# Later transposes of the routing's results, and one-hot operands made one token group ahead, in an expert layer on one core

## The chip, the core and the metric

The kernel runs on 1 core of one Trainium2 chip. The metric is the device time of one execution in microseconds (us), median of several runs. Engines are named as in the profile: PE is TensorE's matmuls and PEld its weight loads, DVE is VectorE, ACT is ScalarE, POOL is GpSimd, SP is SyncE, which issues the weight transfers here.

## The reference

Two transformer layers on one sequence of 256 tokens with 1,024 features. What matters here is the last part, an expert layer with 16,384 experts, of which each token uses 16 for each of 8 heads:

```
q = (h @ w_query).reshape(B, S, 8, 2, 128)
s1, s2 = q[..., 0, :] @ sub_keys1.T, q[..., 1, :] @ sub_keys2.T
v1, i1 = top_k(s1, 16);  v2, i2 = top_k(s2, 16)
cand = v1[..., :, None] + v2[..., None, :]       # 256 candidates
top_v, pos = top_k(cand, 16)
expert_idx = (i1 * 128 + i2) at pos              # routing's places
gates = softmax(top_v)
act = gelu(h . expert_down[expert_idx])
out = sum(gates * act * expert_up[expert_idx])
```

## The kernel before

The kernel computes the expert layer densely: every expert for every token, with a gate that is zero for experts a token did not choose. `peer` runs two stages. The stage of `down` has 64 pairs `jj` of expert tiles; a pair is 2 tiles of 128 experts, each contracted over 8 blocks of features. `mm3` writes three matmuls for each block (L96, L97, L98: high part by high, by low, and low by high), so a pair has 48 matmuls named `dn`. The stage of `up` follows, 128 tiles into four accumulators (`upp`).

Weights are streamed. SP loads a tile (`eraw`, 512 KB), ACT casts it to the high half (`whi`, L69), DVE subtracts to get the low half (`wlo`, L71), four times for a pair. The pool of `whi` and `wlo` has 4 buffers each, which is one pair. `g.mark` is the last of the first 12 `dn` matmuls of the newest pair.

Between the pairs two other things are issued by the Python loop at the end of `peer`. While `routing` lasts, each pair is followed by three steps of that generator. For each of the 8 heads it makes scores (`sps`), the two top-16 lists and the 256 candidates' top 16 on DVE (L1156 to L1204), and puts the two halves of the places into `gts[tt]` (`rk`, L1204), where `tt` is one of the two halves of the tokens. After the last head, for each `tt`, it makes the softmax (L1210 to L1215), and then, once a further pair has been issued, three transposes on PE (`slp`, L1223). ACT and DVE copy them into `slots` as 16-bit numbers (L1225 to L1227): places i1 and i2, and the gate in a high and a low part.

When `routing` has ended, each pair is followed by one or two calls of `gates()`. A call treats a group of NG = 8 tokens, 32 groups in all. It makes `eq` (two instructions, L1301: is this slot's place equal to j) and `gt` (two, L1303: the second of them times the gate) on DVE, 128x1024 each and 16 bits wide, from pools with 2 buffers. It then multiplies them on PE (`gps`, L1309, 16 matmuls into two PSUM tiles of 4 tokens), which gives the gates of all experts for those tokens. For expert tiles that `down` has already done, DVE multiplies the gates into `act` (L1314). For the others, ACT copies them there (L1316), and a later `down` multiplies (L1283, L1284).

`dn`, `gps`, `slp` and `sps` share the PSUM pool `aux` with 5 buffers. A planner fixes each engine's order of instructions when the program is built (`schedule_with_timeline_sim=True`): it follows its own estimate of when each instruction becomes ready, and `after(...)` only gives it an order to keep.

The pairs at which things are issued follow from the code. A head takes 12 steps, that is 4 pairs, so the heads' steps end after pair 30. The softmax of `tt` = 0 is issued after pair 31, its transposes after pair 32; the softmax of `tt` = 1 after pair 32, its transposes after pair 33. Gates start after pair 34: two calls after each of the pairs 34, 35 and 36, one after each of the pairs 37 to 62.

Of the kernel before, what the change touches and what calls it, by code (L numbers as in the profile page):

```python
# [20 lines left out]
T = 256  # L21
# [118 lines left out]
def after(g, ins, first):  # L140

    g.tc.add_manual_dep(ins, first.name, mybir.DependencyInfo(mybir.DependencyClass.NoSync, mybir.DependencyReason.DATA),
                        reason="table order")
# [10 lines left out]
def load(g, dst, src):  # L154

    after(g, g.nc.sync.dma_start(dst, src).ins, g.pm)
# [932 lines left out]
def advance(gen, n):  # L1089

    return sum(next(gen, g) is not g for g in [gen] * n) > 0
# [49 lines left out]
def routing(g, a, q_banks, rp, cp, slots):  # L1141

    nc = g.nc

    rk = rp.tile([P, 1296], F32, tag="rk", name="rk")
    keys = rk[:, 0:256].rearrange("p (a b) -> p a b", a=2)
    io16 = rk[:, 256:272]
    val = [rk[:, 272 + t * 128:400 + t * 128].rearrange("p (a b) -> p a b", a=8) for t in range(2)]  # L1150
    gts = [rk[:, 528 + t * 384:912 + t * 384].rearrange("p (a b) -> p a b", a=3) for t in range(2)]
    load(g, keys, a["keys"])
    load(g, io16, a["c_io16"])

    def top16(src, n, v, i):
        nc.vector.max(v[:, 0:8], src)  # L1156
        nc.vector.max_index(i[:, 0:8], v[:, 0:8], src)
        r = rp.tile([P, 256], F32, tag="rep", bufs=2, name="rep")
        nc.vector.match_replace(r[:, :n], v[:, 0:8], src, -3.0e38)
        nc.vector.max(v[:, 8:16], r[:, :n])  # L1160
        nc.vector.max_index(i[:, 8:16], v[:, 8:16], r[:, :n])

    for h, bank in enumerate(q_banks):
        q = rp.tile([P, 2, T], F32, tag="q", bufs=2, name="q")
        nc.scalar.copy(q, bank)
        m0 = g.mark
        yield
        while g.mark is m0:
            yield
        ps = g.aux.tile([P, 2, 2, 128], F32, tag="aux", name="sps")  # L1170
        for tt in range(2):
            for i in range(2):
                m = nc.tensor.matmul(ps[:, tt, i, :], q[:, i, tt * P:(tt + 1) * P], keys[:, i, :], start=True, stop=True)  # L1173
                if tt + i == 0 and g.mark is not None:
                    after(g, m.ins, g.mark)
        s = rp.tile([P, 2, 2, 128], F32, tag="s", bufs=2, name="s")
        nc.scalar.copy(s, ps)
        yield
        for tt in range(2):
            v = rp.tile([P, 2, 16], F32, tag="v", bufs=2, name="v")  # L1180
            idx = rp.tile([P, 2, 16], U32, tag="idx", bufs=2, name="idx")
            for i in range(2):
                top16(s[:, tt, i, :], 128, v[:, i, :], idx[:, i, :])
                yield
            cand = rp.tile([P, 16, 16], F32, tag="cand", bufs=2, name="cand")
            nc.vector.tensor_tensor(cand, v[:, 0, :].unsqueeze(2).broadcast_to([P, 16, 16]),
                                    v[:, 1, :].unsqueeze(1).broadcast_to([P, 16, 16]), op=ALU.add)
            pos = rp.tile([P, 16], U32, tag="pos", bufs=2, name="pos")
            top16(cand.rearrange("p a b -> p (a b)"), 256, val[tt][:, h, :], pos)
            yield  # L1190

            pi = rp.tile([P, 2, 16], U32, tag="pi", bufs=2, name="pi")
            nc.vector.tensor_scalar(pi[:, 0, :], pos, 4, None, op0=ALU.logical_shift_right)
            nc.vector.tensor_scalar(pi[:, 1, :], pos, 15, None, op0=ALU.bitwise_and)
            pf = rp.tile([P, 2, 16], F32, tag="pf", bufs=2, name="pf")
            nc.vector.tensor_copy(pf, pi)
            xf = rp.tile([P, 2, 16], F32, tag="xf", bufs=2, name="xf")
            nc.vector.tensor_copy(xf, idx)
            eq = rp.tile([P, 2, 16, 16], F32, tag="eq", bufs=2, name="eq")
            nc.vector.tensor_tensor(eq.rearrange("p i k a -> p (i k) a"),  # L1200
                                    pf.rearrange("p i k -> p (i k)").unsqueeze(2).broadcast_to([P, 32, 16]),
                                    io16.unsqueeze(1).broadcast_to([P, 32, 16]), op=ALU.is_equal)
            nc.vector.tensor_tensor(eq, eq, xf.unsqueeze(2).broadcast_to([P, 2, 16, 16]), op=ALU.mult)
            nc.vector.tensor_reduce(gts[tt][:, 0:2, h * 16:h * 16 + 16], eq, axis=AX.X, op=ALU.add)  # L1204
            yield
    for tt in range(2):

        gt = gts[tt]
        e = rp.tile([P, 8, 16], F32, tag="e", bufs=1, name="e")
        nc.vector.tensor_tensor(e, val[tt], val[tt][:, :, 0:1].broadcast_to([P, 8, 16]), op=ALU.subtract)  # L1210
        nc.scalar.activation(e, e, AF.Exp)
        sm = rp.tile([P, 8], F32, tag="sm", bufs=1, name="sm")
        nc.vector.tensor_reduce(sm, e, axis=AX.X, op=ALU.add)
        nc.vector.reciprocal(sm, sm)
        nc.vector.tensor_tensor(gt[:, 2, :].rearrange("p (h k) -> p h k", k=16), e,  # L1215
                                sm.unsqueeze(2).broadcast_to([P, 8, 16]), op=ALU.mult)
        m0 = g.mark
        yield
        while g.mark is m0:
            yield  # L1220
        ps = g.aux.tile([P, 3, 128], F32, tag="aux", name="slp")
        for i in range(3):
            after(g, nc.tensor.transpose(ps[:, i, :], gt[:, i, :], g.ident).ins, g.mark)  # L1223
        ts = slice(tt * P, (tt + 1) * P)
        nc.scalar.copy(slots[:, 0:2, ts], ps[:, 0:2, :])  # L1225
        nc.vector.tensor_scalar(slots[:, 2, ts], ps[:, 2, :], 2.0 ** 14, None, op0=ALU.mult)
        nc.vector.scalar_tensor_tensor(slots[:, 3, ts], ps[:, 2, :], 2.0 ** 14, slots[:, 2, ts], op0=ALU.mult,  # L1227
                                       op1=ALU.subtract)
        yield


def peer(g, a, xT, out):
# [3 lines left out]
    with ExitStack() as es:  # L1236
# [22 lines left out]
        NG = 8  # L1259
        done = [0, 0]  # L1260

        def parts(lo, hi):
            for p in range(2):
                l, h = max(lo, p * H0), min(hi, H0 + p * (NJ - H0))
                if l < h:
                    if act[p] is None:
                        act[p] = ap.tile([P, NJ - H0, T], F32, name="act1")
                    yield act[p], l - p * H0, h - p * H0, l, h
# [17 lines left out]
                nc.scalar.activation(A[:, l:h, tg:], ps[:, :, tg:], AF.Gelu_apprx_tanh)  # L1286
            done[0] += 2

        def gates():

            t0 = done[1]

            shape = [P, NG // 2, 128, 2]

            def slot(i):
                return slots[:, i, t0:t0 + NG].rearrange("p (a b) -> p a b", b=2).unsqueeze(2).broadcast_to(shape)

            eq = wk.tile([P, 2] + shape[1:], F16, tag="eq", name="eq")
            gt = wk.tile([P, 2] + shape[1:], F16, tag="gt", name="gt")
            for i in range(2):  # L1300
                nc.vector.tensor_tensor(eq[:, i], iota.unsqueeze(1).broadcast_to(shape), slot(i), op=ALU.is_equal)  # L1301
            for i in range(2):
                nc.vector.tensor_tensor(gt[:, i], eq[:, 1], slot(2 + i), op=ALU.mult)  # L1303
            for t4 in range(0, NG, 4):
                ps = g.aux.tile([P, 4, 128], F32, tag="aux", name="gps")
                for t in range(4):
                    pr, o = divmod(t4 + t, 2)
                    for i in range(2):
                        nc.tensor.matmul(ps[:, t, :], eq[:, 0, pr, :, o], gt[:, i, pr, :, o], start=i == 0, stop=i == 1)  # L1309
                pj = ps.rearrange("p t j -> p j t")  # L1310
                ts = slice(t0 + t4, t0 + t4 + 4)
                for A, l, h, gl, gh in parts(0, done[0]):
                    A = A[:, l:h, ts]
                    nc.vector.scalar_tensor_tensor(A, pj[:, gl:gh, :], 2.0 ** -14, A, op0=ALU.mult, op1=ALU.mult)  # L1314
                for A, l, h, gl, gh in parts(done[0], NJ):
                    nc.scalar.activation(A[:, l:h, ts], pj[:, gl:gh, :], AF.Copy, scale=2.0 ** -14)  # L1316
            done[1] += NG
# [51 lines left out]
        for jj in range(NJ // 2):  # L1369
            down(jj)  # L1370
            if not advance(rt, 3) and jj <= last:
                for _ in range(-(-((T - done[1]) // NG) // (last + 1 - jj))):
                    gates()
        xn = cp.tile([P, 2, D], F32, name="xn")
# [137 lines left out]
```

## Time and profile before

| | before |
|---|---|
| median of 3 runs | 1463.34 us (1461.71 to 1465.68) |
| the profiled execution's own time | 1462.46 us |
| its span, first to last instruction | 1460.6 us |
| PE busy | 1420.6 us (97%) |
| DVE busy | 1140.0 us (78%) |
| ACT busy | 807.8 us (55%) |
| mean granted clock of TensorE | 0.992 |

The span is what the trace shows; 1.86 us of the profiled execution lie around it. Matmuls overlap, so PE's busy share is high even where it does not go at its best rate; what a matmul costs in a run of them is the step from one start to the next. The stage of `down` lasts from about 641 us to 1100 us, the stage of `up` from there to 1453 us.

### The profile page before, as it was taken

How to read it: one execution, taken by the hardware profiler on the slowest of the kernel's cores; microseconds unless marked ns; L12 is line 12 of the kernel's file. 1: busy time of each engine (PE TensorE's matmuls, PEld its weight loads, DVE VectorE, ACT ScalarE, POOL GpSimd, SP SyncE). 2: the span in 40 equal slices, each digit the busy share in tenths (PEclk: the TensorE clock that was granted, in tenths of full speed). 3: DMA queues.
4: the chain of work that ended last, by engine and by line, in shares of the span. 5: the costliest groups of instructions: out<-in, count | busy, mean ns of one | idle time of the engine just before them, and what ended most of it. 6: DMA issues, size and time to landing. Idle time of an engine off the chain costs nothing.

```text
span 1460.6 us, 29215 instructions
## 1 busy us (share of the span) xinstructions
PE 1420.6 (97%) x11284; PEld 1321.2 (90%) x11284; DVE 1140.0 (78%) x2462; ACT 807.8 (55%) x1613; POOL 46.8 (3%) x45
## 2 busy tenths in 40 slices
PE   7999999998999999989999998999999999999997
PEld 6999999998888888989999998999998888888886
DVE  7769679688878875979988988989996666666665
ACT  6655556645755445555555555555446555555553
POOL 3012011000000000000000000000000000000001
PEclk9999999999999999999999999999999999999999
DMA  7667645787443233545555554445445556565553
GB/s 249 211 190 225 200 135 168 268 271 233 139 150 102 93 118 115 189 135 187 175 184 177 174 174 135 152 148 161 158 159 168 194 194 196 188 199 190 193 196 130
DMA packets 73578, 256.42 MB, mean 176 GB/s; under 512 B 9184, under 2 KB 10848, under 8 KB 73440
## 3 DMA queue, kind: packets, MB, share of 16 engines
q1 hardware_dynamic: 73440, 254.57, 53.9%
q8 instruction: 88, 1.44, 0.4%
q14 instruction: 50, 0.41, 0.1%
HBM read 253.49 MB, written 1.05 MB: 174 GB/s over the span
## 4 chain that ended last, share of the span: by engine, by line
PE 54%; DVE 2%; issue 0%; POOL 0%; POOLq 0%; DVEq 0%
PE dn L96 8%; PE dn L98 8%; PE dn L97 8%; PE upp L1336 8%; PE upp L1337 8%; PE upp L1340 8%; PE gps L1309 2%; PE pj L97 1%; PE pj L98 1%; PE pj L96 1%; PE sps L1173 0%; DVE wlo L71 0%; DVE eq L1301 0%; DVE gt L1303 0%; PE gtp L1357 0%
## 5 line engine op out<-in xcount | busy, mean ns | idle before, releaser
L69 ACT CAST whi<-eraw 128x512 fp32r<-128x512 f32 x512 | 318.1, 622 | 336.7 <-PE upp L1337 146.5
L71 DVE TENSOR_TENSOR wlo<-eraw,whi 128x512 fp32r<-128x512 f32 x512 | 349.5, 687 | 164.6 <-ACT whi L69 163.7
L69 ACT CAST whi<-wraw 128x512 fp32r<-128x512 f32 x336 | 205.9, 619 | 180.8 <-PE pj L97 104.3
L71 DVE TENSOR_TENSOR wlo<-wraw,whi 128x512 fp32r<-128x512 f32 x336 | 238.1, 720 | 73.9 <-ACT whi L69 69.7
L96 PE MATMUL dn<-h3h,whi 128*128 128x256 f32 x1024 | 293.2, 286 | 0.0
L98 PE MATMUL dn<-h3h,wlo 128*128 128x256 f32 x1024 | 291.3, 285 | 0.0
L97 PE MATMUL dn<-h3l,whi 128*128 128x256 f32 x1024 | 290.3, 284 | 0.0
L97 PEld LDWEIGHTS dn<-h3l,whi 128*128 128x128 f32 x1024 | 197.1, 192 | 0.0
L96 PEld LDWEIGHTS dn<-h3h,whi 128*128 128x128 f32 x1024 | 197.1, 192 | 0.0
L98 PEld LDWEIGHTS dn<-h3h,wlo 128*128 128x128 f32 x1024 | 196.8, 192 | 0.0
L1337 PE MATMUL upp<-whi,wl 128*128 128x512 f32 x512 | 158.7, 390 | 0.0
L1340 PE MATMUL upp<-wlo,wh 128*128 128x512 f32 x512 | 157.7, 389 | 0.0
L97 PE MATMUL pj<-hl,whi 128*128 128x256 f32 x496 | 141.1, 286 | 2.3 <-DVE hl L59 2.3
L98 PE MATMUL pj<-hh,wlo 128*128 128x256 f32 x496 | 141.0, 287 | 1.8 <-DVE wlo L71 1.8
L96 PE MATMUL pj<-hh,whi 128*128 128x256 f32 x496 | 141.0, 286 | 1.7 <-ACT whi L69 1.7
L1336 PE MATMUL upp<-whi,wh 128*128 128x512 f32 x512 | 138.5, 390 | 0.0
L1340 PEld LDWEIGHTS upp<-wlo,wh 128*128 128x128 f32 x512 | 96.1, 188 | 20.0
L1337 PEld LDWEIGHTS upp<-whi,wl 128*128 128x128 f32 x512 | 95.8, 188 | 19.8
L1336 PEld LDWEIGHTS upp<-whi,wh 128*128 128x128 f32 x512 | 95.7, 188 | 19.6
L97 PEld LDWEIGHTS pj<-hl,whi 128*128 128x128 f32 x496 | 95.5, 193 | 3.5 <-DVE hl L59 3.3
L98 PEld LDWEIGHTS pj<-hh,wlo 128*128 128x128 f32 x496 | 95.2, 193 | 2.9 <-DVE wlo L71 2.6
L96 PEld LDWEIGHTS pj<-hh,whi 128*128 128x128 f32 x496 | 95.5, 193 | 2.2 <-ACT whi L69 1.9
(477 smaller groups left out, 2723.0 us busy)
## 6 DMA issues: line engine op xcount, KB each, us to landing
eraw<-in_e_down_dram SPq DMA_DIRECT2D x128, 512.0 KB, 3.8
eraw<-in_e_up_dram SPq DMA_DIRECT2D x128, 512.0 KB, 3.6
wraw<-in_w_in_dram SPq DMA_DIRECT2D x80, 512.0 KB, 4.1
adaw<-in_w_ada_dram SPq DMA_DIRECT2D x48, 512.0 KB, 5.2
wraw<-in_w_out_dram SPq DMA_DIRECT2D x16, 512.0 KB, 3.8
wraw<-in_w_gate_dram SPq DMA_DIRECT2D x16, 512.0 KB, 4.0
wraw<-in_w_query_dram SPq DMA_DIRECT2D x16, 512.0 KB, 4.2
wraw<-in_w_rkv_dram SPq DMA_DIRECT2D x12, 512.0 KB, 4.5
```

What stands on the lines that cost most here:

```text
L69: nc.scalar.copy(hi[:, :m], raw[:, o:o + m])
L71: nc.vector.tensor_tensor(lo[:, :m], raw[:, o:o + m], hi[:, :m], op=ALU.subtract)
L96: nc.tensor.matmul(out, lh, rh, start=start, stop=False)
L97: nc.tensor.matmul(out, lh, rl, start=False, stop=False)
L98: return nc.tensor.matmul(out, ll, rh, start=False, stop=stop)
L1309: nc.tensor.matmul(ps[:, t, :], eq[:, 0, pr, :, o], gt[:, i, pr, :, o], start=i == 0, stop=i == 1)
L1336: nc.tensor.matmul(o, wh[:, ts], hi, start=J == 0, stop=False)
L1337: nc.tensor.matmul(o, wl[:, ts], hi, start=False, stop=False)
L1340: nc.tensor.matmul(up_ps[2 * tt + d0 // 4], wh[:, ts], lo, start=False, stop=J == NJ - 1)
```

## The change

Both edits concern the order of work, and the amount of arithmetic stays as it is.

- In `routing`, the wait for a newer pair between the softmax and the transposes of each `tt` is done twice. The transposes of `tt` = 0 are issued after pair 33 (before: 32), the softmax of `tt` = 1 after pair 33 (32), and its transposes after pair 35 (33), behind the first 12 matmuls of that pair.
- `gates()` is split: `operands(t0)` makes `eq` and `gt` of a group and puts them on a list. The first call of it takes the place of gates after pair 36. From then on `gates()` takes the operands of its group from the list, first issues those of the next group, and then does its own matmuls and multiplications.

With this the gates start after pair 37 (before: 34). The loop spreads the 32 groups over the pairs that are left: two after each of the pairs 37 to 42 (six pairs; before three), one after each of the pairs 43 to 62. The pools keep their numbers of buffers.

```diff
-        m0 = g.mark
-        yield
-        while g.mark is m0:
+        for _ in range(2):
+            m0 = g.mark
             yield
+            while g.mark is m0:
+                yield
         ps = g.aux.tile([P, 3, 128], F32, tag="aux", name="slp")
...
-        def gates():
-
-            t0 = done[1]
+        ready = []
+
+        def operands(t0):
 
             shape = [P, NG // 2, 128, 2]
...
             for i in range(2):
                 nc.vector.tensor_tensor(gt[:, i], eq[:, 1], slot(2 + i), op=ALU.mult)
+            ready.append((eq, gt))
+
+        def gates():
+
+            t0 = done[1]
+            eq, gt = ready.pop(0)
+            if t0 + NG < T:
+                operands(t0 + NG)
             for t4 in range(0, NG, 4):
...
             if not advance(rt, 3) and jj <= last:
+                if not done[1] and not ready:
+                    operands(0)
+                    continue
                 for _ in range(-(-((T - done[1]) // NG) // (last + 1 - jj))):
                     gates()
```

## Rows read from the trace of the kernel before

**Rows 1.** Head of the page.
```profile
span 1460.6 us, 29215 instructions
```

**Rows 2.** Waits of PE in 893 to 1101 us and whole span: us in total, times, longest.
```profile
PE slp L1223 <- DVE rk L1204: 4.7, 1, 4.7
PE gps L1309 <- DVE gt L1303: 0.6, 2, 0.3
```

**Rows 3.** Timeline of PE, 874 to 906 us: start, length, instruction, idle time before it.
```profile
879.07 0.49 PE L1223 MATMUL slp<-perm,rk 128*128 128x128 f32 x3
...
887.54 0.28 PE L97 MATMUL dn<-h3l,whi 128*128 128x256 f32 x1
887.66 0.28 PE L98 MATMUL dn<-h3h,wlo 128*128 128x256 f32 x1
892.65 0.87 PE L1223 MATMUL slp<-perm,rk 128*128 128x128 f32 x3 [4.71 <-DVE rk L1204]
...
900.54 2.01 PE L1309 MATMUL gps<-gt,eq 128*128 128x128 f16 x32
```

**Rows 4.** Stretches of 2 us: length, busy PE, PEld, DVE, ACT, POOL, clock, DMA.
```profile
890.00:892.00 2.00, 0.00 (x0) 0.00 (x0) 1.97 (x5) 0.00 (x0) 0.00 (x0) 0.50 0.80 266
...
894.00:896.00 2.00, 2.00 (x11) 2.00 (x11) 0.54 (x2) 0.10 (x1) 0.00 (x0) 0.50 0.00 0
```

**Rows 5.** Timeline of DVE, 874 to 906 us.
```profile
881.17 2.48 DVE L1301 TENSOR_TENSOR eq<-iota,slots 128x1024 f16<-128x1024 f16 x4
...
887.13 1.28 DVE L1303 TENSOR_TENSOR gt<-eq,slots 128x1024 f16<-128x1024 f16 x2
...
891.81 0.69 DVE L1204 TENSOR_REDUCE rk<-eq 128x32 f32<-128x512 f32 x1
```

**Rows 6.** Instructions on the tile dn alone, by stretch (PE, PEld, ACT).
```profile
640.00:888.00 248.00, 202.09 (x1632) 198.33 (x1632) 19.53 (x33) 1.00 0.54 174
```

**Rows 7.** Timeline of DVE, 896 to 946 us.
```profile
901.88 1.28 DVE L1301 TENSOR_TENSOR eq<-iota,slots 128x1024 f16<-128x1024 f16 x2
903.09 1.51 DVE L1314 SCALAR_TENSOR_TENSOR act<-gps,act 128x280 f32<-128x280 f32 x4
...
910.63 1.28 DVE L1301 TENSOR_TENSOR eq<-iota,slots 128x1024 f16<-128x1024 f16 x2
...
925.16 1.28 DVE L71 TENSOR_TENSOR wlo<-eraw,whi 128x512 fp32r<-128x512 f32 x2
```

**Rows 8.** Timelines of PE, three stretches between 908 and 928 us.
```profile
908.20 2.01 PE L1309 MATMUL gps<-gt,eq 128*128 128x128 f16 x32
...
916.44 0.96 PE L1309 MATMUL gps<-gt,eq 128*128 128x128 f16 x14 [0.31 <-DVE gt L1303]
917.74 0.28 PE L1309 MATMUL gps<-gt,eq 128*128 128x128 f16 x2 [0.33 <-DVE gt L1303]
...
927.33 0.36 PE L98 MATMUL dn<-h3h,wlo 128*128 128x256 f32 x1
```

**Rows 9.** Groups of DVE's instructions, 901.88 to 919.44 us: busy, mean ns, idle before.
```profile
L71 DVE TENSOR_TENSOR wlo<-eraw,whi 128x512 fp32r<-128x512 f32 x9 | 5.9, 682 | 0.7 <-ACT whi L69 0.7
...
L1301 DVE TENSOR_TENSOR eq<-iota,slots 128x1024 f16<-128x1024 f16 x8 | 5.1, 680 | 0.0
```

**Rows 10.** Stretches of 2 and 20 us; the columns are those of rows 4.
```profile
916.00:918.00 2.00, 1.36 (x19) 1.09 (x18) 2.00 (x4) 1.15 (x3) 0.00 (x0) 1.00 0.01 2
...
920.00:940.00 20.00, 20.00 (x198) 19.60 (x197) 20.00 (x39) 11.25 (x34) 0.00 (x0) 1.00 0.49 156
940.00:960.00 20.00, 20.00 (x192) 19.74 (x191) 17.58 (x32) 10.76 (x30) 0.00 (x0) 1.00 0.44 144
```

**Rows 11.** Timeline of ACT, 874 to 906 us.
```profile
904.52 1.05 ACT L1316 ACTIVATE act<-gps 128x104 f32<-128x104 f32 x6
```

## The prediction

> **What bounds the kernel now.** I read the head of the page first, then PE's waits, then PE's and DVE's timelines around the longest of them that the change touches. All sums below are made against the profiled execution: its span is 1460.6 us [rows 1], its own time 1462.46 us, that is 0.88 us under the median of the runs, 1463.34 us.
>
> PE is the engine that sets the time of the expert layer. The list of its waits shows only two entries from 893 us to the end of the `down` stage and one large one just before: 4.7 us in which the transposes `slp` waited for L1204 on DVE, and 0.6 us in which `gps` waited for `gt` [rows 2]. Everywhere else in this stage `dn` matmuls follow each other every 0.12 us (887.54 to 887.66, [rows 3]), so a pair of 48 takes 5.76 us. A gain can come from those two waits alone.
>
> The reader is to see where the large wait stands. Up to 888 us PE had run 1632 `dn` matmuls, which is 34 pairs exactly [rows 6], so the waiting transposes are those of `tt` = 1, issued after pair 33 and stuck ahead of pair 34. What they waited for, L1204, starts on DVE at 891.81 us and takes 0.69 us [rows 5]: PE goes on at 892.65 us. DVE wasn't idle before that. From 881.17 us on it made four `eq` and then four `gt`, the operands of the first two groups, whose matmuls came only at 900.54 us [rows 5, 3]. At 0.60 us each (901.88 to 903.09 us for two, [rows 7]) these eight took 4.8 us ahead of the last steps of the routing.
>
> The wait cost more than its own length. The granted clock fell to 0.50 (1.2 GHz) during the idle time and was still there at 894 to 896 us [rows 4]. The whole loss: pair 34 should have begun at 887.66 + 0.12 us and ended 5.76 us later, plus at most 0.49 us for three transposes, the length that the earlier three show [rows 3]. That is 894.03 us; the matmuls behind pair 34 start at 900.54 us [rows 3]. So 6.5 us.
>
> **The change, part by part.** *Transposes later.* Those of `tt` = 0 move from pair 32 into pair 33 behind its twelfth matmul, those of `tt` = 1 into pair 35 behind its twelfth. On the new time scale pair 35 starts at about 893.5 us, so the second set can't be wanted before 893.5 + 12 x 0.12 = 895.0 us. L1204 ended at 892.50 us even with all eight operand instructions ahead of it [rows 5], so it is 2.5 us early at worst. The wait goes, with its clock: -6.5 us. The instructions themselves (three transposes, one copy on ACT, two on DVE, for each `tt`) are moved and not removed, and no transfer and no SP instruction is among them; they count nothing. The softmax of `tt` = 1 comes a pair later, with the same margin of two pairs ahead of its transposes.
>
> *Gates three pairs later.* The same 32 groups now stand among 26 pairs (before 29), and six pairs carry two groups where three did. PE's work doesn't change. DVE's does not either: the gates' multiplications get longer by the expert tiles already done, and the multiplications in `down` get shorter by the tokens not yet gated; both differences are the same 432 elements by the code. But DVE gets less time for it. After the first two groups, it needs 901.88 to 910.63 us, 8.75 us, for all that belongs to a pair with two groups (eight operands, four multiplications, four `wlo`) [rows 7], with 0.7 us idle in two such periods, all of it ahead of a `wlo` [rows 9]. PE needs 900.54 to 908.20 us, 7.66 us [rows 3, 8]. DVE falls behind by 1.09 us for each such pair. Before, the first such interval was covered by operands made early. In the third pair PE waited: its `gps` came in pieces, at 916.44 and 917.74 us, both on `gt` [rows 8]. DVE was then busy for 20.00 of the 20 us from 920 to 940 us and found idle time again only from 940 us on (17.58 of 20, [rows 10]). So the stretch was just long enough to be carried.
>
> With three more such pairs DVE is behind by a further 3 x 1.09 = 3.3 us. Two things can take this in: `wlo` made ahead, and `gps` put later among the `dn` matmuls, which the planner already did. The trace shows what is left of the first at the tightest place I found, pair 38: the `wlo` of 925.16 us ends at about 925.85 us, and the matmul that reads it starts at 927.33 us [rows 7, 8], so 1.5 us. The bounds are nothing (all 3.3 us hidden by `gps` put later) and 3.3 us (nothing hidden; up to 5 us if short waits also break up PE's runs as in rows 8). I take 3.3 - 1.5 = 1.8 us, because the nearest row, the third pair, shows that a lag past the lead does become a wait.
>
> *Operands one group ahead.* This adds no instruction and takes away no buffer. `eq` and `gt` have 2 buffers, so operands of a group can't be made before the `gps` of two groups earlier are done, and the planner had already made the first two groups' operands some 19 us ahead of use [rows 5, 3]. What is new is the order in which they are offered to DVE: the next group's ahead of this group's multiplications. I cost it at nothing; cover is in what follows `gps`: DVE's multiplications began at 903.09 us, behind two `eq` only [rows 7]. If all eight operands went first they would begin 6 x 0.60 = 3.6 us later. Their PSUM tiles were free when ACT's last copies ended, at about 905.6 us [rows 11], 2.6 us before the next `gps` at 908.20 us [rows 8]. So this is worth between nothing and 1.0 us on PE for each pair with two groups.
>
> Here a rule of the Trainium skill speaks against the change: "PSUM — Partial Sum Buffer", section "Engine vs sequencer instructions", has the queues of ScalarE and VectorE as strictly first in, first out, and its section on bank collisions says that two engines' accesses to one PSUM bank are kept apart in time. By that rule ACT's copies of a `gps` tile must wait for DVE's multiplication of the same tile, which stands behind whatever DVE was given first. The timeline agrees as far as order goes, since ACT's copies end after DVE's multiplications. By the rule at its full price the sum would lose the 1.0 us per pair; by the row of the first pair, nothing.
>
> *Sum:* -6.5 + 1.8 = -4.7 us. Span 1455.9 us, own time 1457.8 us, and from the median 1463.34 - 4.7 = 1458.6 us.
>
> **The rivals.** *Hidden stretch.* The planner puts `gps` later and DVE keeps `wlo` flowing, as after 918 us, where DVE was full and PE waited no more. Then the gain is 6.5 us and, if the third pair's waits go too (from 916.44 and 917.74 us they come to 1.0 us by start to start), 7.5 us: 1455.8 to 1456.8 us. For it: no wait of PE on DVE stands in the list after 918 us [rows 2, 8]. Against it: six pairs in a row have no example.
>
> *The wait moves.* Operands ahead of multiplications hold the five PSUM buffers, and `gps` or the next `dn` waits for one: 1.0 us in each of the five intervals between six pairs, beside the 1.8 us, is 6.8 us, about all that is won: 1463.6 us. For it: DVE has no slack there [rows 10]. Against it: only one group's operands are offered ahead, not two.
>
> *Slower: the clock in the two-group stretch.* If DVE's lag is paid in one wait for each of the pairs 37 to 42 and each is long enough to lower the clock, each pair pays the 1.09 us of lag plus what the half clock cost behind the wait of pair 34, 6.5 - 4.7 = 1.8 us. That is 6 x 2.9 = 17.4 us, less 6.5 us gained: 10.9 us slower, 1474.2 us. It decides from a wait about as long as that of pair 34; with waits of a third of a microsecond the clock stood at 1.00 [rows 8, 10], which speaks against it. The Trainium skill ("TensorE: Matmul & The Clock Gate", "A second HAM failure mode: psum-queue depth-cycling") has frequent short idles between groups of matmuls make the clock swing; the trace so far doesn't agree.
>
> **How the numbers follow.** A measurement of this kernel can tell about 0.3%, 4.4 us, from no change. Forecast (extra waits of about 0.7 to 3.3 us, a gain of 3.2 to 5.8 us): 0.42, of which 0.25 lies beyond 0.3%. Hidden stretch: 0.27, all faster. The wait moves: 0.21, the same. Slower: 0.10. So faster 0.52, same 0.38, slower 0.10. The range takes in the hidden stretch at its best, 1455.8 us, and the moved wait with a margin: 1455.5 to 1464.5 us.
>
> **What would show it.** Right: PE's list of waits has no `slp`; the granted clock stays at 1.00 from 880 to 1100 us; the first `gps` follow pair 37 at about 911 us, with operands long ready; DVE is full from there to beyond 950 us, and PE has some short waits on `gt`, `wlo` or a PSUM tile between 925 and 960 us; the `up` stage starts 4 to 5 us earlier than 1100 us. Wrong: a new wait of several us at `gps` or `dn` in that stretch, or one ahead of `upp` because the last gates come late, or time lost outside the expert layer by another plan of the earlier stages.

## The result and the profile after

The changed kernel takes 1469.68 us (median of 6 runs, 1468.29 to 1473.31), the kernel before 1462.13 us beside it (6 runs, 1461.37 to 1465.68): a ratio of 1.0052, 95% interval 1.0040 to 1.0063. It is slower by 0.5%, where 1458.6 us and a range of 1455.5 to 1464.5 us were forecast. The mechanism is near that of the rival "Slower: the clock in the two-group stretch", at two places and not at six.

The head of the page after, with the busy time of each engine, against [rows 1]; the profiled execution's own time is 1469.64 us. PE and DVE have as much work as before, on 7.0 us more span:

```profile
span 1467.6 us, 29215 instructions
...
PE 1422.0 (97%) x11284; PEld 1322.8 (90%) x11284; DVE 1140.7 (78%) x2459; ACT 807.2 (55%) x1610; POOL 48.7 (3%) x45
```

PE's waits of the kernel after from 864 to 1110 us, against [rows 2]. The `slp` entry is gone, and another has come that is nearly twice as large:

```profile
PE gps L1318 <- DVE gt L1304: 8.8, 2, 4.6
```

PE's timeline after, against [rows 3, 8]. The transposes of `tt` = 1 start at 895.93 us with no wait and the first `gps` at 911.85 us. From the start of the last `sps` to that point it takes 52.6 us, with 38 pairs done. Before it was 42.0 us, with 35 pairs done, and three more at 5.76 us would make 59.3 us. So 6.7 us are won by here, where 6.5 were forecast. Then a block of `gps` breaks off after 16 matmuls at 927.22 us, and another at 957.39 us:

```profile
895.93 0.49 PE L1224 MATMUL slp<-perm,rk 128*128 128x128 f32 x3
...
911.85 2.02 PE L1318 MATMUL gps<-gt,eq 128*128 128x128 f16 x32
...
927.22 1.09 PE L1318 MATMUL gps<-gt,eq 128*128 128x128 f16 x16
932.50 0.39 PE L1318 MATMUL gps<-gt,eq 128*128 128x128 f16 x2 [4.18 <-DVE gt L1304]
...
933.01 0.41 PE L97 MATMUL dn<-h3l,whi 128*128 128x256 f32 x1
933.22 0.41 PE L98 MATMUL dn<-h3h,wlo 128*128 128x256 f32 x1
...
935.78 0.41 PE L98 MATMUL dn<-h3h,wlo 128*128 128x256 f32 x1
...
937.07 1.41 PE L1318 MATMUL gps<-gt,eq 128*128 128x128 f16 x14
...
941.71 2.01 PE L1318 MATMUL gps<-gt,eq 128*128 128x128 f16 x32
...
957.39 1.09 PE L1318 MATMUL gps<-gt,eq 128*128 128x128 f16 x16
963.06 0.39 PE L1318 MATMUL gps<-gt,eq 128*128 128x128 f16 x2 [4.58 <-DVE gt L1304]
...
972.35 1.09 PE L1318 MATMUL gps<-gt,eq 128*128 128x128 f16 x16
```

The two lone `gps` stand at the head of PE's queue, and every `dn` behind them waits along. When PE goes on, `dn` steps are 0.21 us (933.01 to 933.22) and not 0.12, and the granted clock is 0.50 (next rows). From one block of `gps` to the next it takes 941.71 - 927.22 = 14.49 us and 972.35 - 957.39 = 14.96 us, where the prediction's 7.66 us is the undisturbed length: both stretches hold 32 `gps` and 48 `dn`, as that one does. That is 6.8 + 7.3 = 14.1 us lost, 8.8 of it in the waits and 5.3 behind them.

Stretches of the kernel after (length, busy PE, PEld, DVE, ACT, POOL, clock, DMA), against [rows 4, 10]. DVE is busy for 2.00 of 2 us while PE has nothing, so it isn't waiting for anything:

```profile
928.00:930.00 2.00, 0.31 (x6) 0.14 (x3) 2.00 (x4) 0.82 (x4) 0.00 (x0) 1.00 0.22 43
930.00:932.00 2.00, 0.00 (x0) 0.00 (x0) 2.00 (x6) 0.60 (x4) 0.00 (x0) 0.79 0.90 317
...
934.00:936.00 2.00, 2.00 (x12) 2.00 (x11) 0.24 (x1) 0.57 (x1) 0.00 (x0) 0.50 0.00 0
...
938.00:940.00 2.00, 2.00 (x22) 2.00 (x20) 1.93 (x4) 1.28 (x5) 0.00 (x0) 1.00 0.00 0
```

DVE's timeline after, ahead of the first of the two waits and behind it, against [rows 7]:

```profile
925.83 0.87 DVE L1323 SCALAR_TENSOR_TENSOR act<-gps,act 128x312 f32<-128x312 f32 x2
926.61 1.28 DVE L1302 TENSOR_TENSOR eq<-iota,slots 128x1024 f16<-128x1024 f16 x2
927.81 1.89 DVE L71 TENSOR_TENSOR wlo<-eraw,whi 128x512 fp32r<-128x512 f32 x3
929.62 1.29 DVE L1302 TENSOR_TENSOR eq<-iota,slots 128x1024 f16<-128x1024 f16 x2
930.82 0.88 DVE L1323 SCALAR_TENSOR_TENSOR act<-gps,act 128x320 f32<-128x320 f32 x2
931.62 0.21 DVE L1285 TENSOR_TENSOR act<-act,gl 128x64 f32<-128x64 f32 x1
931.75 2.49 DVE L1304 TENSOR_TENSOR gt<-eq,slots 128x1024 f16<-128x1024 f16 x4
936.08 0.69 DVE L71 TENSOR_TENSOR wlo<-eraw,whi 128x512 fp32r<-128x512 f32 x1 [1.83 <-ACT whi L69]
938.07 0.93 DVE L1323 SCALAR_TENSOR_TENSOR act<-gps,act 128x320 f32<-128x320 f32 x2 [1.31 <-PE gps L1318]
```

Two `eq` are made at 926.61 us. The `gt` that belong to them, which PE wants at about 928 us, come at 931.75 us, behind three `wlo` and behind the two `eq` of the next group at 929.62 us. Below this is called a late `gt`. The kernel after has it at both places where PE waits. The three `wlo` weren't urgent: counted in order, the first of them is read by the `dn` at 935.78 us, 7.3 us after it is done.

Behind the wait DVE itself runs out of work, for 1.83 and 1.31 us, and the same again behind the second wait. The whole stretch from the first block of two groups to the end of the sixth is 60.50 us long (columns as above), where PE's undisturbed 6 x 7.66 us are 46.0:

```profile
911.85:972.35 60.50, 51.62 (x482) 50.60 (x480) 53.50 (x100) 25.77 (x83) 0.00 (x0) 0.89 0.31 105
```

So 14.5 us are lost in it. DVE is busy for 53.5 us, 7.5 more than PE would need undisturbed, and idle for 7.0.

The account: -6.7 us for `slp`, -1.0 us for the third pair's waits of before [rows 8], which aren't there now, +14.1 us for the two stalls and +0.4 us for the block between them with a small gap at 950.6 us make +6.8 us. The stage from the start of the last `sps` to that of the first `upp` measures 241.81 us before and 248.10 us after: +6.3 us. From the first `upp` to the end it is 360.2 us in both traces. The other 0.7 us lie ahead of the first `dn`, which starts between 639.1 and 645.7 us in the traces of this document. The time of this one stage is therefore given with each run below, from its one trace.

### The profile page after: what moved, and what is told of

It reads as the page before. It is cut to its first block, busy times and chain, and to the rows that moved or that the text cites. A ratio compares the mean times of both kernels' runs of the same rounds, so it can differ in the third digit from the quotient of the medians.

```text
span 1467.6 us, 29215 instructions
## 1 busy us (share of the span) xinstructions
PE 1422.0 (97%) x11284; PEld 1322.8 (90%) x11284; DVE 1140.7 (78%) x2459; ACT 807.2 (55%) x1610; POOL 48.7 (3%) x45
## 3 DMA queue, kind: packets, MB, share of 16 engines
q1 hardware_dynamic: 73440, 254.57, 53.5%
```

## The experiments

Three theories. **Load:** a pair with two groups gives DVE 8.75 us of work and PE 7.66 us, and six in a row let DVE fall further behind than `wlo` made ahead can cover. **Order:** DVE would be in time, but a late `gt` holds up PE. **Operands ahead:** issuing the next group's `eq` and `gt` ahead of this group's multiplications makes the waits. In the expectations A is the order, B the load and C the operands ahead. The kernel before took 1462.5 us (median) beside `late_only`, `ahead_only`, `spread` and `order`, 1462.79 us beside `pool`, `late1`, `late1_spread` and `late_spread`, and 1462.9 us beside the other three.

**One part at a time.** `late_only` has the first hunk of the change alone; its gates start after pair 36 and five pairs in a row have two groups:

```diff
-        m0 = g.mark
-        yield
-        while g.mark is m0:
+        for _ in range(2):
+            m0 = g.mark
             yield
+            while g.mark is m0:
+                yield
```

> The transposes wait for a second pair as in the change, the operands are made as before; gates start after pair 36 and five pairs in a row carry two groups. Theory A (order on DVE): the loss comes where the planner puts a group's gt behind three wlo, the next group's eq and multiplications, each time worth about 7 us (a wait of 4 to 5 us and a half clock behind it). This kernel has that order at one place, the changed kernel at two. So the gain of 6.5 us at slp less one loss of 7 us: no change, about 1462 us. Theory B (load on DVE): the loss grows by the number of pairs with two groups whatever the order, 1.09 us of lag each beyond the second plus what the clock takes. Five pairs instead of six: about 1466 us. If the operands made ahead are the cause (theory C): 1456 us.

Measured: 1462.12 us, ratio 0.9990 (0.9979 to 1.0002), stage 239.50 us. PE's waits from 860 to 1110 us in `late_only`:

```profile
PE gps L1310 <- DVE gt L1304: 4.3, 1, 4.3
```

So one long wait, with one late `gt` ahead of it, and no operands made ahead. The long wait doesn't need the second hunk. The time is the one forecast by order (1462 us); load by itself gave 1466 us.

`ahead_only` has `operands`, its list and the loop's new branch, with the transposes where they were; four pairs in a row have two groups:

```diff
...
+            eq, gt = ready.pop(0)
+            if t0 + NG < T:
+                operands(t0 + NG)
...
```

> Operands one group ahead, transposes as before; gates start after pair 35 and four pairs in a row carry two groups. The wait of 4.7 us at slp stays. Theory A: no place with the late gt, so about the time before, 1462 us. Theory B: one more pair with two groups than before, 1.1 us: 1463 us. Theory C: operands ahead cost what was seen, about 13 us: 1475 us.

Measured: 1465.22 us, ratio 1.0016 (1.0006 to 1.0027), stage 243.69 us. The wait of `slp` is still there with the same 4.7 us, so the second hunk wins nothing of it, and with four pairs in a row there are more waits on `gt` than the 0.6 us of before:

```profile
PE gps L1317 <- DVE gt L1303: 2.7, 3, 1.5
```

The 1475 us of theory C didn't come. The time is some 2 us above what load forecast (1463 us) and 3 above order (1462 us).

**The pairs with two groups spread out.** `spread` is the change with the six of them apart; all else is as in the kernel after:

```diff
-                for _ in range(-(-((T - done[1]) // NG) // (last + 1 - jj))):
+                for _ in range(2 if jj in (40, 44, 48, 52, 56, 60) else 1):
```

> The changed kernel, but the six pairs with two groups are 40, 44, 48, 52, 56 and 60 instead of 37 to 42. Theories A and B: both big waits of PE on gt go, the gain at slp stays: 6.5 to 7.5 us under the time before, about 1455 us. Theory C: the waits stay, about 1469 us.

Measured: 1458.64 us, ratio 0.9970 (0.9959 to 0.9980), stage 236.98 us: 11.1 us less than after, by the loop's count alone. That is 3.6 us short of the 1455 us that both theories gave. The waits on `gt` are 1.8 us in two, beyond 1056 us. That speaks for load, since the work and the operands ahead are the same; but order isn't excluded, as the planner may order DVE otherwise here.

**DVE's order laid down.** `order` is the change, and the `eq` of a group may not stand ahead of the `gt` of the group before it on DVE:

```diff
-                nc.vector.tensor_tensor(eq[:, i], ..., op=ALU.is_equal)
+                m = nc.vector.tensor_tensor(eq[:, i], ..., op=ALU.is_equal)
+                if g.gt_last is not None:
+                    after(g, m.ins, g.gt_last)
...
-                nc.vector.tensor_tensor(gt[:, i], eq[:, 1], slot(2 + i), op=ALU.mult)
+                m = nc.vector.tensor_tensor(gt[:, i], eq[:, 1], slot(2 + i), op=ALU.mult)
+            g.gt_last = m.ins
```

> The changed kernel with one order laid down on DVE: the eq of a group stand behind the gt of the group before. The six pairs with two groups stay in a row. Theory A: gt comes some 2 us sooner at the two places, the waits fall from 4.4 and 4.8 us to 2 to 3 us and the clock stays up: about 1461 us. Theory B: the load is the same, so is the time, about 1469 us.

Measured: 1463.6 us, ratio 0.9999 (0.9989 to 1.0010), stage 241.61 us, 6.5 us less than after. PE's waits and three stretches of `order`, the first of them the six pairs with two groups:

```profile
PE gps L1321 <- DVE gt L1306: 5.6, 5, 2.0
```

```profile
913.02:967.10 54.08, 48.48 (x482) 47.25 (x481) 52.95 (x100) 25.59 (x83) 0.00 (x0) 0.97 0.35 116
920.00:940.00 20.00, 17.77 (x188) 17.09 (x188) 20.00 (x39) 9.87 (x31) 0.00 (x0) 1.00 0.32 111
940.00:960.00 20.00, 16.63 (x167) 16.16 (x166) 20.00 (x39) 8.64 (x28) 0.00 (x0) 0.99 0.39 131
```

No `gt` stands behind the next group's `eq` now, DVE has no idle time for 40 us, and PE still waits five times. The six pairs take 54.08 us where 46.0 us would be undisturbed: 8.1 us are lost, 5.6 of them in the waits, and some 1.5 in a stretch at half clock behind the last wait. DVE is busy for 52.95 us of them, so at most 1.1 us could be won by keeping it busier. That is load, as far as it goes. The planner's order brings the lag of several pairs into one wait, long enough for the clock, and DVE then stands idle: the kernel after has 5.9 us more idle time of DVE in these pairs and takes 6.4 us more. So the order theory holds for the step from 1463.6 to 1469.68 us, and not for the loss of the gain.

One order wasn't laid down in any run. Ahead of the longest wait of `order` DVE makes three `wlo` before the `gt` that PE waits for at 958.83 us:

```profile
956.05 1.88 DVE L71 TENSOR_TENSOR wlo<-eraw,whi 128x512 fp32r<-128x512 f32 x3
957.85 0.31 DVE L1285 TENSOR_TENSOR act<-act,gl 128x160 f32<-128x160 f32 x1
958.09 1.28 DVE L1306 TENSOR_TENSOR gt<-eq,slots 128x1024 f16<-128x1024 f16 x2
```

Counted in order, these `wlo` are read 4.9 us or more after they are done. Whether a `gt` put ahead of them would push some of the lag past the end of the stretch stays open.

**Load taken away.** `pool` is the change, with one of the four `wlo` of pairs 38 to 43 made on GpSimd:

```diff
-                for o, hi, lo in halves(g, raw, 1024):
+                for o, hi, lo in halves(g, raw, 1024, (None, 1) if src is a["e_down"] and 38 <= jj <= 43 and j else (None,)):
```

> The changed kernel with its six pairs of two groups in a row, but in the pairs 38 to 43 GpSimd makes one of the four wlo. DVE's work for such a pair falls by 0.60 us to about 8.15 us against 7.66 us of PE; the planner's order then has no gt behind the next group's eq. Load on DVE as the cause of lag: 0.5 us for each pair, waits of 2 us in all or less, about 1457 us. If lag has another source (PSUM tiles): short waits as with the order laid down, 6 us: about 1463 us.

Measured: 1464.1 us, ratio 1.0007 (0.9997 to 1.0018), stage 241.31 us, with six waits of 5.3 us in all. It missed what load forecast, but it is not a clean test, because DVE's own instructions became slower beside GpSimd's. Groups of DVE in `pool`, 914 to 960 us (busy us, mean ns):

```profile
L1304 DVE TENSOR_TENSOR gt<-eq,slots 128x1024 f16<-128x1024 f16 x20 | 14.2, 746 | 0.0
L1285 DVE TENSOR_TENSOR act<-act,gl 128x32 f32<-128x32 f32 x1 | 1.3, 1311 | 0.0
```

and of the kernel after, 914 to 927 us:

```profile
L1304 DVE TENSOR_TENSOR gt<-eq,slots 128x1024 f16<-128x1024 f16 x6 | 3.9, 686 | 0.0
L1285 DVE TENSOR_TENSOR act<-act,gl 128x32 f32<-128x32 f32 x1 | 0.2, 188 | 0.0
```

Six `wlo` less save DVE 6 x 0.6 = 3.6 us. The 20 `gt` alone give back 20 x 0.060 = 1.2 us, the one multiplication 1.1 us, and the 20 `eq` (733 ns in the mean where they took 686) another 0.9 us.

`order_light` takes the load away without another engine: the order laid down, and in pairs 38 to 43 two of four `wlo` not computed; the products there take the high half in their place, so the output lacks these low parts.

```diff
+        if eng[i % len(eng)] == 0:
+            lo = hi
...
+                for o, hi, lo in halves(g, raw, 1024, (None, 0) if src is a["e_down"] and 38 <= jj <= 43 else (None,)):
```

> The kernel with the order laid down (six pairs of two groups in a row), but in the pairs 38 to 43 two of the four wlo are left out: the matmuls read whi in their place, so the low part of the weights is missing there and the result is off, while PE has the same instructions. DVE's work for such a pair falls by 1.2 us, to about 7.6 us against 7.66 us of PE. Load on DVE as the cause of the short waits: they go, 6 us less than with the order alone, about 1457 us. PSUM tiles or the planner's order as their cause: they stay, 1463 us.

Measured: 1456.07 us, ratio 0.9961 (0.9945 to 0.9976), stage 235.04 us, 6.6 us less than `order`. PE's waits in `order_light` are down to

```profile
PE gps L1323 <- DVE gt L1308: 0.2, 1, 0.2
```

and the six pairs with two groups last

```profile
912.01:958.82 46.81, 46.56 (x483) 45.74 (x481) 45.26 (x87) 25.74 (x83) 0.00 (x0) 1.00 0.38 132
```

With 12 x 0.6 = 7.2 us of DVE's work gone, DVE is busy for less than PE's 46.0 us, and 5.4 of 5.6 us of waits are gone, as load forecast (1457 us). There are also fewer `wlo` ahead of a `gt` here, so this run alone doesn't tell load from that order.

`late_order` is `late_only` with the order laid down.

> Both transposes later, operands made as before (five pairs in a row with two groups), and eq of a group laid down behind the gt of the group before. Order on DVE as the cause of the one wait of 4.5 us in the kernel with later transposes alone: that wait falls to about 2 us, with the clock up: 4 to 5 us less than that kernel's 1462.1 us, about 1458 us. Load alone: no change, 1462 us.

Measured: 1460.83 us, ratio 0.9984 (0.9975 to 0.9994), stage 238.98 us, between the two numbers. The 4.3 us of one wait became 3.8 us in four (longest 1.6), and the stage is only 0.5 us shorter than in `late_only`. Order forecast about 1458 us, load 1462 us. Here too the order moves the lag about and hardly lessens it.

**Fewer and wider apart.** `late1` makes only the transposes of `tt` = 1 wait twice, with operands made as before; four pairs in a row have two groups:

```diff
+        for _ in range(1 + tt):
+            m0 = g.mark
             yield
```

> Only the transposes of the second half of the tokens wait for a second pair; operands made as before, gates from pair 35 on, four pairs in a row with two groups, and no place where the planner puts a gt behind the next eq. Order on DVE as the cause: the wait at slp goes (6.5 us) and nothing of 7 us comes; what is left is lag on DVE, short waits of 0.5 to 2 us, about 3 us in all as with operands ahead alone: about 1459 us. Number of pairs with two groups as the cause, whatever the order: four against three before costs 1 to 2 us: 1457 us. Operands ahead or a late start of the gates as the cause: nothing lost, 1456 us.

Measured: 1459.95 us, ratio 0.9979 (0.9967 to 0.9990), stage 236.72 us, waits of 2.0 us in four (longest 0.9) on `gt` and one of 0.6 us on `whi`. The forecast that came true to 1 us is the one by order, with short waits of DVE's lag left (1459 us); the number of pairs by itself gave 1457 us. Against `ahead_only`, which also has four pairs in a row, this shows what operands ahead do there: its stage of 243.69 us less the 6.7 us for `slp` is 237.0 us, the same as here to 0.3 us.

`late1_spread` is `late1` with the pairs of two groups at 40, 46, 52 and 58.

> As the kernel with one later transpose, but the four pairs with two groups are 40, 46, 52 and 58. Lag on DVE as the cause of the short waits: they go, 6.5 to 7.5 us under the time before, about 1455 us. If it is something else in the start of the gates: 1459 us as with four in a row.

Measured: 1458.72 us, ratio 0.9976 (0.9966 to 0.9985), stage 235.94 us. No wait on `gt` is left (2.0 us on other tiles are), but in the time of the kernel this misses the 1455 us. The stage is only 0.8 us shorter than in `late1`.

`late_spread` is `late_only` with two groups after 40, 44, 48, 52 and 56, so it is `spread` without operands made ahead.

> Both transposes later, operands made as before, gates from pair 36 on, the five pairs with two groups are 40, 44, 48, 52 and 56. Against the changed kernel with spread groups this tells what operands ahead are worth by themselves: if nothing, about 1457 to 1458 us; if they help, slower than that kernel's 1458.6 us by 1 us or more.

Measured: 1457.92 us, ratio 0.9966 (0.9951 to 0.9980), stage 235.24 us, one wait of 1.8 us. `spread` took 1458.64 us beside another run of the kernel before, ratio 0.9970 (0.9959 to 0.9980): the intervals overlap almost wholly, so operands ahead are worth nothing that can be measured here (the intervals are 3 to 4 us wide).

`late_alt` has both transposes later, operands as before, and two groups after every third pair:

```diff
+                for _ in range(2 if jj in (37, 40, 43, 46, 49) else 1):
```

> A version meant to beat both: both transposes later, operands made as before, and the five pairs with two groups early and apart (37, 40, 43, 46, 49), before the multiplications by the gates have grown. The wait at slp gone and no wait of more than 1 us behind it: 6.5 to 7.5 us under the time before, about 1455.5 us. If two groups every third pair are still too many for DVE, or the start of the up stage comes late: 1458 us as with every fourth.

Measured: 1455.17 us, ratio 0.9951 (0.9937 to 0.9965), stage 234.68 us. It beats both kernels. PE's list of waits is empty from 860 to 1110 us. Two stretches of `late_alt`:

```profile
920.00:940.00 20.00, 20.00 (x199) 19.70 (x198) 19.04 (x37) 10.28 (x32) 0.00 (x0) 1.00 0.45 153
940.00:960.00 20.00, 20.00 (x199) 19.70 (x199) 20.00 (x38) 10.12 (x29) 0.00 (x0) 1.00 0.45 152
```

PE is full and DVE nearly so, both at once: by this, what a pair with two groups costs DVE too much, the two pairs with one group behind it give back. The order of DVE was left to the planner here.

## Why the prediction was wrong

**The transposes: right.** The wait is gone, the first `gps` follow pair 37 at 911.85 us where about 911 was forecast, and by then 6.7 us are won where 6.5 were forecast. `late_alt` keeps the whole of it: its stage is 241.81 - 234.68 = 7.1 us shorter than before, against the 7.5 us that the prediction gave for `slp` and the third pair together.

**Operands ahead: right at nothing, as far as it was tried.** `spread` and `late_spread` differ by less than their intervals, and the stages with four pairs in a row by 0.3 us. With six in a row it wasn't tried apart from the sixth pair. The moved wait through PSUM tiles didn't come: no such wait is in the list after.

**The failed step** is in the part on gates three pairs later: "Two things can take this in: `wlo` made ahead, and `gps` put later among the `dn` matmuls, which the planner already did", and from it 3.3 - 1.5 = 1.8 us. The lag of one pair was sized well. (The 0.7 us of idle time that the prediction read into two periods stand ahead of a `wlo` at 901.27 us, before the first of them; DVE had none.) But nothing took it in. `order`, where DVE has 1.1 us of idle time and no late `gt`, loses 8.1 us in the six pairs, the kernel after 14.5 us. The lag of all six pairs is 6 x 1.09 = 6.5 us, and 7.0 us by DVE's 52.95 us against PE's 46.0: it is this that was paid whole, and not the lag of the three added pairs less a lead. The lead that was subtracted, 1.5 us of `wlo`, took in nothing, since every wait is on `gt` and the `wlo` ahead of it kept leads of several us. The prediction took what carried the first three pairs before (two groups' operands made early, DVE idle again only from 940 us on, [rows 5, 10]) as if it were still there for three more. With 8.1 us for this term, and the third pair's old waits taken off with those of `slp`, the sum is -7.5 + 8.1 = +0.6 us; the interval of `order` (0.9989 to 1.0010) is -1.6 to +1.5 us. The bound of 3.3 us ("nothing hidden") was too low for the same reason.

**The second part of the failure is the chance of the rival.** It named the clock behind a long wait and its condition, a wait about as long as that of pair 34, and it got 0.10, since the waits seen until then were a third of a microsecond. The kernel after has such waits, 4.18 and 4.58 us, at two places, so the loss is 14.1 us in place of the rival's 17.4 us, and the time 1469.68 us in place of 1474.2 us. That the two losses are so near is in part luck: the rival had six waits of 1.09 us each with its clock. What the prediction lacked is that lag can gather: the planner put the `gt` of one group behind the `eq` of the next and behind `wlo` made early, and DVE, 2.00 of 2 us busy, paid several pairs' lag ahead of one `gps`. Three pairs' lag and the next group's two `eq` would be 3 x 1.09 + 2 x 0.60 = 4.5 us, and the two waits, three pairs apart, are 4.18 and 4.58 us; that split is argued and not shown, and the three `wlo` (1.8 us) could stand in it as well. `order` shows what this gathering costs, 1469.68 - 1463.6 = 6.1 us.

Why PE waits for a `gt` so long in two of the six pairs, and not in the other four, is open; the planner's estimates weren't tried. Whether more buffers for `eq` and `gt` would carry the lag wasn't tried either.

## What to carry to other kernels

When a change makes a stretch of work denser, compare the periods of the two engines in that stretch, and take the lag times the whole number of repeats, not only those added. What covered the stretch before (work made early, an idle gap behind it) covers it once. Spreading the dense steps so that the slower engine catches up between two of them won 0.5% here, where reordering the same work won nothing over the kernel before.

## What was unexpected of the hardware

**The clock can fall after PE has gone on.** PE's timeline in `order`, around the longest of its waits:

```profile
931.67 0.29 PE L1321 MATMUL gps<-gt,eq 128*128 128x128 f16 x2 [1.73 <-DVE gt L1306]
...
958.83 0.29 PE L1321 MATMUL gps<-gt,eq 128*128 128x128 f16 x2 [2.05 <-DVE gt L1306]
...
959.48 0.41 PE L97 MATMUL dn<-h3l,whi 128*128 128x256 f32 x1
959.69 0.41 PE L98 MATMUL dn<-h3h,wlo 128*128 128x256 f32 x1
```

and stretches of `order`:

```profile
958.00:960.00 2.00, 1.18 (x9) 1.18 (x10) 2.00 (x5) 0.00 (x0) 0.00 (x0) 0.87 0.80 266
960.00:962.00 2.00, 2.00 (x11) 2.00 (x11) 2.00 (x5) 0.91 (x5) 0.00 (x0) 0.50 0.67 225
```

After a wait of 2.05 us PE starts with its `gps` at full speed (0.29 us for two), and some half microsecond later the `dn` step is 0.21 us (959.48 to 959.69) and the granted clock 0.50 (1.2 GHz). The wait of 1.73 us left the clock at 1.00. In `late_only` the clock was still 1.00 while PE stood idle for 4.30 us, and fell as it went on:

```profile
934.00:936.00 2.00, 0.00 (x0) 0.00 (x0) 2.00 (x6) 0.59 (x4) 0.00 (x0) 1.00 0.87 320
936.00:938.00 2.00, 1.46 (x9) 1.47 (x10) 2.00 (x4) 0.20 (x2) 0.00 (x0) 0.68 0.44 168
938.00:940.00 2.00, 2.00 (x11) 2.00 (x11) 0.30 (x2) 0.62 (x1) 0.00 (x0) 0.50 0.00 0
```

In the kernel after it fell during a wait of about the same length (0.79 at 930 to 932 us). So here a wait of 2.05 us was already followed by a stretch at half clock, and the place where it was paid lay behind the wait.

**DVE is slower beside GpSimd.** In `pool` the mean `gt` took 746 ns where it took 686 in the kernel after, one 128x32 multiplication 1311 ns where it took 188, and GpSimd's 128x512 `wlo` took 1.28 to 4.61 us. The shortest and the longest:

```profile
914.65 1.28 POOL L73 TENSOR_TENSOR wlo<-eraw,whi 128x512 fp32r<-128x512 f32 x1 [282.31 <-ACT whi L69]
...
940.03 4.61 POOL L73 TENSOR_TENSOR wlo<-eraw,whi 128x512 fp32r<-128x512 f32 x1 [5.29 <-ACT whi L69]
```

The Trainium skill ("SBUF — State Buffer", section "Who interferes with whom") says that DVE and GpSimd share one pair of SBUF ports and that one of them locks it against the other. These rows agree with that: of the 22 `gt` of `pool` from 914 to 967 us, the 11 that overlap a `wlo` of GpSimd took 825 ns in the mean, the other 11 took 678 ns. No run here singles the ports out as the cause.
